# A transformer layer on one Trainium2 core: the last five steps of the kernel by halves of columns, with its final norm rearranged

## The chip, the core and the metric

The kernel runs as one program on one core of a Trainium2 chip. The metric is the device time of one execution in microseconds (us); lower is better. The core's engines work side by side and wait for each other through semaphores: TensorE (PE in the profile; its weight loads are PEld), VectorE (DVE), ScalarE (ACT), GpSimd (POOL) and the queues that issue DMAs. Here SyncE's queue (SP) issues nearly all loads and half of the stores, ACT's queue the other stores.

## The reference

One layer on 1024 frames of width 1024, in float32. Only the last two lines are touched by the change, but the program is one.

```python
h = rms_norm(x, norm1); P = h @ w_in
A = forgetting_attention(...)        # 8 heads, causal, with forget gates
B = chunk_band_attention(...)        # 8 heads, own chunk and 8 before it
x = x + (sigmoid(gA) * (A @ w_a) + sigmoid(gB) * (B @ w_b)) @ w_out
h2 = rms_norm(x, norm2)
x = x + square(relu(h2 @ w_up)) @ w_down       # 1024 -> 4096 -> 1024
return rms_norm(x, final_norm)
# rms_norm(x, g) = x * rsqrt(mean(x * x) + 1e-6) * g, mean over the 1024 features
```

## The kernel before

**Layout.** Activations lie with the features on the 128 partitions and the frames along the free dimension. Frames come in two halves of 512 columns, h = 0 and h = 1 (`HALF = 512`). The output `outT` has eight rows of 128 features; a row of one half is 128x512 floats, 256 KB.

**Exact products.** Every float32 operand is split into a high part (rounded to fp32r) and a low part (the rest), and a product is three matmuls: high by high, high by low, low by high. The high parts are ACT casts (`wh`, `xT4h`), the low part of a weight is a POOL subtraction (`wl`, line 165), that of an activation a DVE subtraction (`xT4l`).

**The down projection** (`w_down`) is the last stage. It is done by Strassen's scheme in seven products in the order of `STEPS`: A11, S1, S2, S3, S4, A12, A22. Each has 16 steps k = 0..15, and a step multiplies one weight quarter (128x512: four blocks m of 128 output features) by one activation tile (128x512): 4 x 3 = 12 matmuls into four PSUM banks `dA22_0..3`. A22 is the last; its activation is T4, read from DRAM (`a_dram`), its weight comes from `wall`.

**Operands of a step** are made by `prepare(s)`: the activation is loaded on SP (`xT`), cast on ACT and subtracted on DVE; then the weight of the step two later (`WLEAD = 2`) is loaded on SP (`wr`); then this step's weight is cast on ACT and subtracted on POOL. From step `GSTEPS` on these instructions keep the order in which they are written on their engines (wrapper class `Ordered`: VO, TO, AO, LO; the profile gives them line 106, the wrapper's line). So the SP queue holds `xT(s), wr(s+2), xT(s+1), wr(s+3)` and so on. There are four buffers for `wr` (`RAW = 4`): the load for step s+2 waits until POOL has subtracted the weight of step s-2. There are six for raw `xT` (`XR`), four each for `xT4h` and `xT4l` (`XB`), six each for `wh` and `wl` (`HL`). `prepare` is called up to three steps ahead (`LEAD`).

**The last steps of A22** are split by columns: with `STAG = 2`, the steps k = 13, 14, 15 are held back and done for the first 256 columns, bank by bank (m = 0..3, three steps each), then for the other 256 columns. After a bank's half: DVE adds it onto `accu` (line 1277), `final` squares the sum on ACT, adds the square onto the running sum on DVE (line 233; the sums lie in `rstd`, named `accs`), and scales `accu` by the norm's gain on ACT (line 1173). Four output rows are in `accu` (tile `au`), four in `accp` (tile `p1`, complete before these steps).

**The final norm of a half of columns** is `finish`: `norm_stat` sums the squares over the partitions by two matmuls with a column of ones (PSUM tile `n_s`), `rms` and `newton` make the inverse root (ACT square root into `n_r`, then small DVE instructions), `spread` copies it to all partitions by two matmuls with the identity (PSUM tile `n_b`), and then eight tiles are multiplied by it and stored. In the first 256 columns of h = 0 POOL multiplies all eight, from an SBUF copy that ACT makes, and SP stores them by pairs; in the second DVE multiplies all eight, straight from PSUM, and SP and ACT take turns to store. The half h = 1 is finished earlier, during A12, with DVE and POOL taking turns; SP's loads for A22 stand behind the first of its stores.

Of the kernel before, what the change touches and what calls it, by code (L numbers as in the profile page):

```python
# [44 lines left out]
LAST_HEAD = "FFFFMWTHTFFFLHFTPLTWPHMLFFWFFTHHLMLTPFFHLTVFXFHLPPMOOTHLOPPOPWVXOO"  # L45
FILL_FROM = 9

LEAD, XB, XR = 3, 4, 6

WLEAD = 2  # L50

STAG = 2

GSTEPS = 4

# [37 lines left out]
def hybrid_block(ctx: ExitStack, tc: tile.TileContext, xT, xN, g1, wall, wf, fb, relb, g2, g3, outT):  # L93
# [28 lines left out]
    def tmp(name, dt=F32):  # L122
        return tp.tile([P, HALF], dt, tag="t", name=name, bufs=8)
# [108 lines left out]
            A.activation(sq, src, AF.Square)  # L232
            eng.tensor_tensor(acc, acc, sq, op=ALU.add)

    def newton(name, v, y, t=None):

        if t is None:
            t = cpool.tile([P, 8], F32, tag="nt", name=f"{name}_t", bufs=2)[:, :v.shape[1]]
        V.reciprocal(y, y)
        V.tensor_tensor(t, v, y, op=ALU.mult)  # L240
        V.tensor_tensor(t, t, y, op=ALU.mult)
        V.tensor_scalar(t, t, -0.5, 1.5, op0=ALU.mult, op1=ALU.add)
        V.tensor_tensor(y, y, t, op=ALU.mult)

    def spread(ps_pool, name, y, eng=T):

# [11 lines left out]
        newton("n1", v, y)  # L258
        return [y[:, 4 * h:4 * h + 4] for h in range(2)]

    def norm_stat(ps_pool, name, acc, eng=T):

        ps = ps_pool.tile([P, HALF], F32, tag="d", name=f"{name}_s")
        n = acc.shape[1] // P
        for c in range(n):
            eng.matmul(ps[:, c:c + 1], acc[:, c * P:(c + 1) * P], ones, start=True, stop=True)
        return rms(name, ps, n)

    def rms(name, ps, n=4):

        y, v, t = cpool.tile([P, 2, 4], F32, tag="nr", name=f"{name}_r", bufs=2)[:, 0, 0:n], ps[:, 8:8 + n], ps[:, 16:16 + n]
        V.tensor_scalar(v, ps[:, 0:n], EPS, None, op0=ALU.add)
        A.activation(y, ps[:, 0:n], AF.Sqrt, bias=epsb)
        newton(name, v, y, t)
        return y

    def split(dst, src, eng):
# [894 lines left out]
        begun.add(h)  # L1172
        A.activation(dst, dst, AF.Copy, scale=gt[:, 2, m + 4 * row:m + 4 * row + 1])

    def finish(ps_pool, h, tiles, engs, q=0, w=HALF):

        cols = slice(q * w, (q + 1) * w)
        eng = T if h else TO
        y = norm_stat(ps_pool, f"n3_{h}{q}", accs[h][:, cols], eng)
        yield  # L1180
        if h:
            yield
        pb = spread(ps_pool, f"n3_{h}{q}", y, eng)[:, 0:w]
        scale = accs[h][:, cols]
        if G in engs:
            A.copy(scale, pb)
        yield
        n = 0
        for row, t in enumerate(tiles):
            for m in range(4):  # L1190
                dst = t[:, m, cols]
                if engs[n % len(engs)] is G:
                    G.tensor_tensor(dst, dst, scale, op=ALU.mult)
                else:
                    V.tensor_tensor(dst, dst, pb, op=ALU.mult)
                out = outT[:, :, h * HALF + q * w:h * HALF + (q + 1) * w]
                if engs != (G,):
                    (load, store)[n % 2](out[:, m + 4 * row, :], dst)
                elif m % 2:
                    load(out[:, m + 4 * row - 1:m + 4 * row + 1, :], t[:, m - 1:m + 1, cols])  # L1200
                n += 1
                yield

    def between(n, banks):

        for m in range(4):
            at = lambda t: t[:, m, :]
            total = lambda t, src: V.tensor_tensor(at(t), banks[m], at(src), op=ALU.add)
            if n == "A11":
                A.copy(at(p1), banks[m])  # L1210
            elif n == "S1":
                total(av, p1)
            elif n == "S2":
                total(au, p1)
                yield
                total(av, av)
            elif n == "S3":
                total(aw, av)
                yield
                total(au, au)  # L1220
            elif n == "S4":
                total(av, av)
                final(av, m, 0, 1)
                yield
                final(aw, m, 1, 1)
            else:
                total(p1, p1)
                final(p1, m, 0, 0)
            yield
        for t, row, h in {"S2": ((p1, 0, 0),), "S3": ((aw, 1, 1), (av, 0, 1), (au, 1, 0))}.get(n, ()):  # L1230
            for m in range(4):
                residual(t, m, row, h)
                if m % 2:
                    yield
        if n == "S4":
            yield from finish(psm[0], 1, (av, aw), (V, G))

    def prepare(s):
        _, n, x, k = steps[s]
# [16 lines left out]
    for s, (i, n, x, k) in enumerate(steps):  # L1256
# [9 lines left out]

        if n == "A22" and k == 15 - STAG:

            for _ in rest:
                pass  # L1270
            rest, w = iter(()), HALF // 2
            for q in range(2):
                cols = slice(q * w, (q + 1) * w)
                for m in range(4):
                    for k in range(15 - STAG, 16):
                        multiply(m, k, cols)
                    V.tensor_tensor(au[:, m, cols], banks[m][:, cols], au[:, m, cols], op=ALU.add)
                    final(au, m, 1, 0, cols)
                    if m % 2:
                        next(rest, None)  # L1280
                for _ in rest:
                    pass
                rest = finish(psm[1], 0, (p1, au), (V,) if q else (G,), q, w)
            break
        for m in range(4):
            multiply(m, k)
# [60 lines left out]
```

## Time and profile before

| | |
|---|---|
| median of 3 runs | 1427.55 us (1426.97 to 1428.85) |
| the profiled execution | 1430.48 us, of which the profile's span is 1428.5 us |
| TensorE busy | 1400.7 us (98% of the span), weight loads 1168.7 us |
| VectorE, ScalarE, GpSimd busy | 885.1 us, 706.6 us, 812.2 us |
| mean granted TensorE clock | 0.995 |
| moved from and to HBM | 172.70 MB read, 85.69 MB written |

Times in the profile are microseconds from the start of the span. A row of the timeline gives the start, the duration, the engine, the source line, the operation, "out<-in" by the program's tile names with buffer numbers left out, and in square brackets how long the engine was idle before and what released it. A busy TensorE is not a TensorE at its peak, since matmuls overlap: what tells its pace is the distance from one start to the next.

### The profile page before, as it was taken

To read this page: it belongs to the slowest core of one execution; us is meant where nothing else is said; L and a number is where in the kernel's file an instruction comes from. 1 tells how busy PE (TensorE), PEld (TensorE's weight loads), DVE (VectorE), ACT (ScalarE), POOL (GpSimd) and SP (SyncE) were. 2 spreads that over 40 slices of the span, in tenths; PEclk is the share of its full clock that TensorE was granted. 3 is DMA by queue.
4 is the path that set the end of the run, shared out by engine and by line. 5 is a ranking of instruction groups with operands and counts; after the bars stand their busy time and mean duration, and the time that the engine had idled before them with its cause. 6 is when DMAs were issued, how large, how long until landed. Compare 5 with 4: busy or idle time off the path is not lost.

```text
span 1428.5 us, 20411 instructions
## 1 busy us (share of the span) xinstructions
PE 1400.7 (98%) x6676; PEld 1168.7 (82%) x6676; DVE 885.1 (62%) x1389; ACT 706.6 (49%) x1361; POOL 812.2 (57%) x639
## 2 busy tenths in 40 slices
PE   9999999999999999999999999999999999999996
PEld 6788888888878888888888888888888888888885
DVE  7756445543258887776655855545555559998644
ACT  8534333343358887775454543333333444444653
POOL 0477777778832233113724677777777545567564
PEclk9999999999999999999999999999999999999998
DMA  8546667773454668886644244444444784678263
GB/s 282 154 116 194 187 196 219 204 198 121 147 169 147 185 209 248 246 257 215 213 162 146 68 166 151 155 154 157 148 154 169 252 269 156 178 234 225 81 221 118
DMA packets 132820, 259.75 MB, mean 182 GB/s; under 512 B 18594, under 2 KB 20642, under 8 KB 129642
## 3 DMA queue, kind: packets, MB, share of 16 engines
q1 hardware_dynamic: 84570, 172.79, 38.6%
q10 hardware_dynamic: 44944, 77.78, 17.2%
q0 software_dynamic: 3200, 7.88, 2.5%
q8 instruction: 52, 0.85, 0.2%
q14 instruction: 54, 0.44, 0.1%
HBM read 172.70 MB, written 85.69 MB: 181 GB/s over the span
## 4 chain that ended last, share of the span: by engine, by line
PE 87%; DVE 3%; issue 3%; ACT 2%; POOL 2%; DMA 2%; SPq 0%; POOLq 0%; ACTq 0%; DVEq 0%
PE u L216 44%; PE dS L216 12%; PE dA L216 5%; PE o L216 5%; PE s L106 5%; PE pv L106 4%; PE pt L106 3%; PE m L106 3%; PE m L216 3%; POOL wl_A L165 1%; PE u L106 1%; DMA xg<-xT 1%; DMA xT<-a_dram 1%; ACT p L106 1%; PE vtp L627 0%
## 5 line engine op out<-in xcount | busy, mean ns | idle before, releaser
L165 POOL TENSOR_TENSOR wl_A<-wr,wh_A 128x512 fp32r<-128x512 f32 x118 | 158.4, 1352 | 94.0 <-ACT wh_A L163 77.0
L165 POOL TENSOR_TENSOR wl_S<-S,wh_S 128x512 fp32r<-128x512 f32 x102 | 136.0, 1337 | 32.9 <-ACT wh_S L163 32.3
L163 ACT CAST wh_S<-S 128x512 fp32r<-128x512 f32 x105 | 64.6, 621 | 114.0 <-PE u L216 53.9
L163 ACT CAST wh_A<-wr 128x512 fp32r<-128x512 f32 x105 | 65.0, 620 | 88.7 <-PE u L216 55.8
L106 DVE TENSOR_TENSOR tl<-pt,th 128x512 fp32r<-128x512 f32 (+1 forms) x144 | 90.5, 641 | 25.9 <-ACT th L106 24.4
L165 POOL TENSOR_TENSOR wl_S<-ks,wh_S 128x512 fp32r<-128x512 f32 x48 | 69.1, 1501 | 53.4 <-ACT wh_S L106 50.0
L590 DVE TENSOR_TENSOR u<-u,u 128x512 f32<-128x512 f32 x70 | 48.8, 698 | 76.0 <-PE u L216 73.6
L106 ACT ACTIVATE p<-s,mn 128x640 f32<-128x640 f32 (+3 forms) x120 | 84.4, 703 | 16.6 <-DVE mn L106 15.5
L106 ACT CAST th<-pt 128x512 fp32r<-128x512 f32 (+1 forms) x144 | 77.6, 551 | 24.5 <-PE pt L106 22.3
L106 PE MATMUL pt<-ident,p 128*128 128x128 f32 x528 | 78.1, 274 | 1.2 <-DVE zt L403 1.1
L186 POOL TENSOR_TENSOR S<-wr,wr 128x512 f32<-128x512 f32 x35 | 46.3, 1324 | 54.8 <-DMA wr<-wall 50.2
L106 PEld LDWEIGHTS pt<-ident,p 128*128 128x128 f32 x528 | 62.2, 141 | 11.0 <-PE pv L106 2.0
L106 PE MATMUL s<-qk 128*128 128x384 f32 (+2 forms) x192 | 58.6, 360 | 8.1 <-ACT p L106 7.3
L165 POOL TENSOR_TENSOR wl_A<-ka,wh_A 128x512 fp32r<-128x512 f32 x32 | 45.1, 1419 | 35.6 <-ACT wh_A L106 34.1
L278 ACT CAST qkh<-qk 128x512 fp32r<-128x512 f32 x32 | 19.9, 621 | 87.5 <-DMA qk_dram<-qkl 34.2
L1102 ACT ACTIVATE v<-v 128x512 f32<-128x512 f32 x64 | 40.4, 632 | 45.1 <-DVE v L1101 42.9
L924 POOL TENSOR_TENSOR on<-on,lo 128x512 f32<-128x512 f32 x7 | 9.0, 1292 | 92.7 <-ACT lo L106 92.7
L106 PE MATMUL pv<-th,v 128*128 128x512 f32 (+3 forms) x180 | 61.3, 348 | 0.1
L583 DVE TENSOR_TENSOR u<-u,c 128x512 f32<-128x512 f32 x35 | 24.5, 699 | 59.4 <-PE u L216 57.3
L106 PE MATMUL pv<-tl,v 128*128 128x512 f32 (+3 forms) x180 | 56.8, 335 | 0.2 <-DVE tl L106 0.2
L1101 DVE SCALAR_TENSOR_TENSOR v<-u,rstd 128x512 f32<-128x512 f32 x64 | 43.9, 688 | 20.1 <-PE u L216 18.1
L581 DVE TENSOR_TENSOR c<-u,u 128x512 f32<-128x512 f32 x35 | 24.2, 691 | 50.7 <-PE u L216 48.9
(445 smaller groups left out, 4742.2 us busy)
## 6 DMA issues: line engine op xcount, KB each, us to landing
wr<-wall SPq DMA_DIRECT2D x233, 256.0 KB
a_dram<-at ACTq DMA_DIRECT2D x64, 256.0 KB
xT<-a_dram SPq DMA_DIRECT2D x64, 256.0 KB
qk<-qk_dram SPq DMA_DIRECT2D x15, 1024.0 KB
qk_dram<-qkh ACTq DMA_DIRECT2D x96, 128.0 KB
a_dram<-v ACTq DMA_DIRECT2D x48, 256.0 KB
xB<-a_dram SPq DMA_DIRECT2D x44, 256.0 KB
z_dram<-zt ACTq DMA_DIRECT2D x32, 256.0 KB
```

The source lines that it names most:

```text
L106: return lambda *a, **kw: tc.keep_in_program_order(getattr(self.eng, name)(*a, **kw))
L163: (act.tensor_copy if act is G or act is V else act.copy)(wh, src)
L165: lows.append(eng.tensor_tensor(wl, src, wh.bitcast(F32), op=ALU.subtract))
L186: eng.tensor_tensor(t, raw(3), raw(2), op=ALU.add)
L216: done = eng.matmul(bank, w[wi], x[xi], start=(first and t == 0), stop=(t == n - 1 and not part), skip_group_check=part or not first)
L278: A.copy(dst[0], src)
L581: V.tensor_tensor(c22, banks[2], u2, op=ALU.add)
L583: V.tensor_tensor(banks[1], banks[3], c22, op=ALU.add)
L590: V.tensor_tensor(banks[b], banks[b], u2, op=ALU.add)
L924: G.tensor_tensor(o, o, lows_o[pr], op=ALU.add)
L1101: V.scalar_tensor_tensor(v, src, 0.0, rstd[:, hs(h)], op0=ALU.max, op1=ALU.mult)
L1102: A.activation(v, v, AF.Square)
```

## The change

Six things change at once.

1. `STAG` goes from 2 to 4: the steps k = 11 to 15 are done by halves of columns, so five steps per bank instead of three, 120 matmuls of 256 columns instead of 72, and 24 fewer of 512. All five steps' operands must be held at once, and `XB` goes from 4 to 5.
2. The square of the last bank (m = 3) of each half is no longer added onto the running sum on DVE; its sum over the partitions is added in PSUM by two more matmuls with the ones (`more` in `norm_stat`).
3. The first half's inverse root is spread while TensorE is in the second half's bank m = 2, not after the last product. POOL multiplies the four tiles of `accp` and DVE the four of `accu`; the stores are by pairs, one of them on ACT's queue.
4. The second half is multiplied by DVE (six tiles) and POOL (two), after an ACT copy, and stored in five DMAs.
5. `newton` takes four DVE instructions instead of five, in all norms; the epsilon is added after the square root on ACT has been issued, and the mean lies in SBUF.
6. Four matmuls with the identity (`spin`) stand between the second half's sums and its spread.

```diff
@@ -45,11 +45,11 @@
 LAST_HEAD = "FFFFMWTHTFFFLHFTPLTWPHMLFFWFFTHHLMLTPFFHLTVFXFHLPPMOOTHLOPPOPWVXOO"
 FILL_FROM = 9
 
-LEAD, XB, XR = 3, 4, 6
+LEAD, XB, XR = 3, 5, 6
 
 WLEAD = 2
 
-STAG = 2
+STAG = 4
 
 GSTEPS = 4
 
@@ -232,15 +232,14 @@
             A.activation(sq, src, AF.Square)
             eng.tensor_tensor(acc, acc, sq, op=ALU.add)
 
-    def newton(name, v, y, t=None):
+    def newton(name, v, y, t=None, vec=V):
 
         if t is None:
             t = cpool.tile([P, 8], F32, tag="nt", name=f"{name}_t", bufs=2)[:, :v.shape[1]]
-        V.reciprocal(y, y)
-        V.tensor_tensor(t, v, y, op=ALU.mult)
-        V.tensor_tensor(t, t, y, op=ALU.mult)
-        V.tensor_scalar(t, t, -0.5, 1.5, op0=ALU.mult, op1=ALU.add)
-        V.tensor_tensor(y, y, t, op=ALU.mult)
+        vec.reciprocal(y, y)
+        vec.tensor_tensor(t, y, y, op=ALU.mult)
+        vec.scalar_tensor_tensor(t, t, -0.5, v, op0=ALU.mult, op1=ALU.mult)
+        vec.scalar_tensor_tensor(y, t, 1.5, y, op0=ALU.add, op1=ALU.mult)
 
     def spread(ps_pool, name, y, eng=T):
 
@@ -258,20 +257,23 @@
         newton("n1", v, y)
         return [y[:, 4 * h:4 * h + 4] for h in range(2)]
 
-    def norm_stat(ps_pool, name, acc, eng=T):
+    def norm_stat(ps_pool, name, acc, eng=T, more=None):
 
         ps = ps_pool.tile([P, HALF], F32, tag="d", name=f"{name}_s")
         n = acc.shape[1] // P
-        for c in range(n):
-            eng.matmul(ps[:, c:c + 1], acc[:, c * P:(c + 1) * P], ones, start=True, stop=True)
-        return rms(name, ps, n)
-
-    def rms(name, ps, n=4):
-
-        y, v, t = cpool.tile([P, 2, 4], F32, tag="nr", name=f"{name}_r", bufs=2)[:, 0, 0:n], ps[:, 8:8 + n], ps[:, 16:16 + n]
-        V.tensor_scalar(v, ps[:, 0:n], EPS, None, op0=ALU.add)
+        for t in (acc,) if more is None else (acc, more):
+            for c in range(n):
+                eng.matmul(ps[:, c:c + 1], t[:, c * P:(c + 1) * P], ones, start=more is None or (t is acc and c == 0),
+                           stop=more is None or t is more, skip_group_check=more is not None)
+        return rms(name, ps, n, V if more is None else VO)
+
+    def rms(name, ps, n=4, vec=V):
+
+        r = cpool.tile([P, 2, 4], F32, tag="nr", name=f"{name}_r", bufs=2)
+        y, v = r[:, 0, 0:n], r[:, 1, 0:n]
         A.activation(y, ps[:, 0:n], AF.Sqrt, bias=epsb)
-        newton(name, v, y, t)
+        vec.tensor_scalar(v, ps[:, 0:n], EPS, None, op0=ALU.add)
+        newton(name, v, y, ps[:, 16:16 + n], vec)
         return y
 
     def split(dst, src, eng):
@@ -1172,32 +1174,24 @@
         begun.add(h)
         A.activation(dst, dst, AF.Copy, scale=gt[:, 2, m + 4 * row:m + 4 * row + 1])
 
-    def finish(ps_pool, h, tiles, engs, q=0, w=HALF):
-
-        cols = slice(q * w, (q + 1) * w)
-        eng = T if h else TO
-        y = norm_stat(ps_pool, f"n3_{h}{q}", accs[h][:, cols], eng)
+    def finish(ps_pool, h, tiles):
+
+        y = norm_stat(ps_pool, f"n3_{h}", accs[h], T)
         yield
-        if h:
-            yield
-        pb = spread(ps_pool, f"n3_{h}{q}", y, eng)[:, 0:w]
-        scale = accs[h][:, cols]
-        if G in engs:
-            A.copy(scale, pb)
+        yield
+        pb = spread(ps_pool, f"n3_{h}", y, T)
+        scale = accs[h]
+        A.copy(scale, pb)
         yield
         n = 0
         for row, t in enumerate(tiles):
             for m in range(4):
-                dst = t[:, m, cols]
-                if engs[n % len(engs)] is G:
+                dst = t[:, m, :]
+                if n % 2:
                     G.tensor_tensor(dst, dst, scale, op=ALU.mult)
                 else:
                     V.tensor_tensor(dst, dst, pb, op=ALU.mult)
-                out = outT[:, :, h * HALF + q * w:h * HALF + (q + 1) * w]
-                if engs != (G,):
-                    (load, store)[n % 2](out[:, m + 4 * row, :], dst)
-                elif m % 2:
-                    load(out[:, m + 4 * row - 1:m + 4 * row + 1, :], t[:, m - 1:m + 1, cols])
+                (load, store)[n % 2](outT[:, m + 4 * row, h * HALF:(h + 1) * HALF], dst)
                 n += 1
                 yield
 
@@ -1233,7 +1227,7 @@
                 if m % 2:
                     yield
         if n == "S4":
-            yield from finish(psm[0], 1, (av, aw), (V, G))
+            yield from finish(psm[0], 1, (av, aw))
 
     def prepare(s):
         _, n, x, k = steps[s]
@@ -1268,19 +1262,62 @@
 
             for _ in rest:
                 pass
-            rest, w = iter(()), HALF // 2
+            while len(ready) < len(steps):
+                ready.append(prepare(len(ready)))
+            rest, w, tiles, lasts, ys, pbs = iter(()), HALF // 2, (p1, au), [], [], []
+
+            def spin(n):
+                bank = psm[1].tile([P, HALF], F32, tag="d", name="spin")
+                for _ in range(n):
+                    TO.matmul(bank[:, 0:P], ident, ident, start=True, stop=True)
+
+            def stat(q):
+                ys.append(norm_stat(psm[1], f"n3_0{q}", accs[0][:, q * w:(q + 1) * w], TO, lasts[q]))
+
+            def wide(q):
+                pbs.append(spread(psm[1], f"n3_0{q}", ys[q], TO)[:, 0:w])
+
+            def spare(q):
+                A.copy(accs[0][:, q * w:(q + 1) * w], pbs[q])
+
+            def scaled(q, row, ms, eng, queue):
+                cols = slice(q * w, (q + 1) * w)
+                for m in ms:
+                    t = tiles[row][:, m, cols]
+                    eng.tensor_tensor(t, t, accs[0][:, cols] if eng is G else pbs[q], op=ALU.mult)
+                queue(outT[:, 4 * row + ms[0]:4 * row + ms[-1] + 1, cols], tiles[row][:, ms[0]:ms[-1] + 1, cols])
+
             for q in range(2):
                 cols = slice(q * w, (q + 1) * w)
                 for m in range(4):
                     for k in range(15 - STAG, 16):
                         multiply(m, k, cols)
+                        if (q, m, k) == (1, 2, 16 - STAG):
+                            wide(0)
+                            spare(0)
                     V.tensor_tensor(au[:, m, cols], banks[m][:, cols], au[:, m, cols], op=ALU.add)
-                    final(au, m, 1, 0, cols)
-                    if m % 2:
-                        next(rest, None)
-                for _ in rest:
-                    pass
-                rest = finish(psm[1], 0, (p1, au), (V,) if q else (G,), q, w)
+                    if m < 3:
+                        final(au, m, 1, 0, cols)
+                    else:
+                        lasts.append(tmp("sq")[:, 0:w])
+                        A.activation(lasts[q], au[:, m, cols], AF.Square)
+                        A.activation(au[:, m, cols], au[:, m, cols], AF.Copy, scale=gt[:, 2, 7:8])
+                    if q and m == 0:
+                        stat(0)
+                    if q and m == 2:
+                        for ms in ((0, 1), (2, 3)):
+                            scaled(0, 0, ms, G, load)
+            scaled(0, 1, (0, 1), VO, store)
+            scaled(0, 1, (2, 3), VO, load)
+            stat(1)
+            spin(4)
+            wide(1)
+            spare(1)
+            scaled(1, 0, (0, 1), VO, load)
+            scaled(1, 1, (2, 3), G, load)
+            scaled(1, 0, (2, 3), VO, store)
+            scaled(1, 1, (0,), VO, load)
+            scaled(1, 1, (1,), VO, store)
             break
         for m in range(4):
             multiply(m, k)
```

The first place is TensorE where A22's steps go over to halves of columns (`xT4h13` is the high part of the activation of step 13, `wl_A22_13` the low part of its weight, `dA22_0` the bank of m = 0). Before:

```order
L106 MATMUL dA22_3_13924<-xT4h12_14149,wl_A22_12_14157 128x512
L106 MATMUL dA22_0_13921<-xT4h13_14173,wh_A22_13_14179 128x256
L106 MATMUL dA22_0_13921<-xT4l13_14174,wh_A22_13_14179 128x256
L106 MATMUL dA22_0_13921<-xT4h13_14173,wl_A22_13_14181 128x256
L106 MATMUL dA22_0_13921<-xT4h14_14197,wh_A22_14_14201 128x256
L106 MATMUL dA22_0_13921<-xT4l14_14198,wh_A22_14_14201 128x256
L106 MATMUL dA22_0_13921<-xT4h14_14197,wl_A22_14_14203 128x256
L106 MATMUL dA22_0_13921<-xT4h15_14219,wh_A22_15_14223 128x256
L106 MATMUL dA22_0_13921<-xT4l15_14220,wh_A22_15_14223 128x256
L106 MATMUL dA22_0_13921<-xT4h15_14219,wl_A22_15_14225 128x256
L106 MATMUL dA22_1_13922<-xT4h13_14173,wh_A22_13_14179 128x256
```

The whole matmuls of step 12 stand ahead of the first half, and step 15 is the third of the halves. The same engine and place in the changed kernel, from the second matmul of step 12 (the three of step 11 and the first of step 12, all 128x256, stand right ahead of it, and ahead of those the whole matmuls of step 10):

```order
L106 MATMUL dA22_0_13917<-xT4l12_14146,wh_A22_12_14151 128x256
L106 MATMUL dA22_0_13917<-xT4h12_14145,wl_A22_12_14153 128x256
L106 MATMUL dA22_0_13917<-xT4h13_14169,wh_A22_13_14175 128x256
L106 MATMUL dA22_0_13917<-xT4l13_14170,wh_A22_13_14175 128x256
L106 MATMUL dA22_0_13917<-xT4h13_14169,wl_A22_13_14177 128x256
L106 MATMUL dA22_0_13917<-xT4h14_14193,wh_A22_14_14197 128x256
L106 MATMUL dA22_0_13917<-xT4l14_14194,wh_A22_14_14197 128x256
L106 MATMUL dA22_0_13917<-xT4h14_14193,wl_A22_14_14199 128x256
L106 MATMUL dA22_0_13917<-xT4h15_14203,wh_A22_15_14207 128x256
L106 MATMUL dA22_0_13917<-xT4l15_14204,wh_A22_15_14207 128x256
L106 MATMUL dA22_0_13917<-xT4h15_14203,wl_A22_15_14209 128x256
L106 MATMUL dA22_1_13918<-xT4h11_14121,wh_A22_11_14127 128x256
```

The product of step 15 for the bank m = 0 now stands ahead of all products of steps 11 to 14 for the other banks. The orders of SP, ACT, DVE and POOL from A22's first operand to its last are those of before.

The second place is ScalarE at the program's end, from the last square (`sq`) on. Before, and then changed:

```order
L232 ACTIVATE sq_14358<-accu_11375 128x256
L1173 ACTIVATE accu_11375<-accu_11375,gt_77 128x256
L1186 COPY rstd_80<-n3_00_b_14362 128x256
L273 ACTIVATE n3_01_r_14381<-n3_01_s_14378,epsb_73 128x2
L1198 DMA outT<-accp1_11374 128x256 x2
L1198 DMA outT<-accu_11375 128x256 x2
```

```order
L1303 ACTIVATE sq_14388<-accu_11372 128x256
L1304 ACTIVATE accu_11372<-accu_11372,gt_77 128x256
L1288 DMA outT<-accu_11372 128x2x256
L274 ACTIVATE n3_01_r_14402<-n3_01_s_14397,epsb_73 128x2
L1281 COPY rstd_80<-n3_01_b_14414 128x256
L1288 DMA outT<-accp1_11371 128x2x256
L1288 DMA outT<-accu_11372 128x256
```

(`n3_00` is the norm of the first 256 columns, `n3_01` that of the second; `_s` the sums, `_r` the inverse roots, `_b` the spread.) A store of the first half now stands ahead of the second half's square root, and the copy after its spread is new. On VectorE at the same place, from the last bank's addition on in the changed kernel:

```order
L1298 TENSOR_TENSOR accu_11372<-dA22_3_13920,accu_11372 128x256
L106 TENSOR_TENSOR accu_11372<-accu_11372,n3_00_b_14348 128x256 x4
L106 TENSOR_SCALAR n3_01_r_14402<-n3_01_s_14397 128x2
L106 RECIPROCAL n3_01_r_14402<-n3_01_r_14402 128x2
L106 TENSOR_TENSOR n3_01_s_14397<-n3_01_r_14402 128x2
L106 SCALAR_TENSOR_TENSOR n3_01_s_14397<-n3_01_s_14397,n3_01_r_14402 128x2
L106 SCALAR_TENSOR_TENSOR n3_01_r_14402<-n3_01_s_14397,n3_01_r_14402 128x2
L106 TENSOR_TENSOR accp1_11371<-accp1_11371,n3_01_b_14414 128x256 x4
L106 TENSOR_TENSOR accu_11372<-accu_11372,n3_01_b_14414 128x256 x2
```

Before, six small instructions stood there, and then four multiplications of `accp1` and four of `accu`, both by the second half's spread.

## The prediction

> **What bounds the kernel now.** I read the page first, then the waits over the last product A22, then the timelines of its last steps and of the end.
>
> ```profile
> span 1428.5 us, 20411 instructions
> PE 1400.7 (98%) x6676; PEld 1168.7 (82%) x6676; DVE 885.1 (62%) x1389; ACT 706.6 (49%) x1361; POOL 812.2 (57%) x639
> ```
>
> TensorE is busy nearly throughout, so only its waits, and what follows its last product, can be won or lost. First its pace, and where it waits near the end:
>
> ```profile
> 1396.90 0.39 PE L106 MATMUL dA<-xT4h,wh_A 128*128 128x512 f32 x1
> ...
> 1405.06 0.28 PE L106 MATMUL dA<-xT4h,wh_A 128*128 128x256 f32 x1
> ...
> 1407.21 0.38 PE L106 MATMUL dA<-xT4h,wl_A 128*128 128x256 f32 x1 [0.74 <-POOL wl_A L165]
> 1407.43 0.28 PE L106 MATMUL dA<-xT4h,wh_A 128*128 128x256 f32 x1
> 1407.55 0.28 PE L106 MATMUL dA<-xT4l,wh_A 128*128 128x256 f32 x1
> ...
> 1415.34 0.28 PE L106 MATMUL dA<-xT4h,wl_A 128*128 128x256 f32 x1
> 1416.60 0.71 PE L106 MATMUL n_b<-ident,n_r 128*128 128x128 f32 x4 [0.98 <-DVE n_r L243]
> 1417.15 0.52 PE L106 MATMUL n_s<-ones,rstd 128*128 128x1 f32 x4
> 1419.22 0.71 PE L106 MATMUL n_b<-ident,n_r 128*128 128x128 f32 x4 [1.55 <-DVE n_r L243]
> ```
>
> The first row is the first of step 10 (from it on the program order is kept), the second the first of step 13, where the halves begin: 36 matmuls in 8.16 us, 0.227 us each, 2.72 us a step. The halves go at 0.12 us a matmul. The third row is the ninth of the 72: step 15's low weight came late. The last product ends at 1415.62 (call it T0); the span goes on for 12.9 us. What made step 15 late:
>
> ```profile
> ACT xT4h L106 <- DMA xT<-a_dram: 10.8, 7, 3.3
> ACT xT4h L106 <- PE dA L216: 2.6, 2, 1.4
> PEld dA L106 <- POOL wl_A L165: 0.9, 1, 0.9
> PEld dA L106 <- DVE xT4l L106: 0.2, 1, 0.2
> ...
> SPq L106 <- POOL wl_A L165: 17.5, 10, 3.3
> ```
>
> The first four are waits from 1370 to 1408, the last SP's own from 1360 to 1410. The casts wait for loads (7 times), hardly for TensorE to free a buffer (2), and the loads wait in SP's queue for POOL's subtraction (10 times, 17.5 us), which frees a raw weight buffer. The last turn of that loop, from three timelines:
>
> ```profile
> 1397.17 4.71 POOL L165 TENSOR_TENSOR wl_A<-wr,wh_A 128x512 fp32r<-128x512 f32 x3 [2.99 <-ACT wh_A L106]
> ...
> 1398.50 0.33 SPq L106 DMA_DIRECT2D wr<-wall  x1
> 1398.92 0.86 SPq L106 DMA_DIRECT2D xT<-a_dram  x2
> ...
> 1402.97 0.62 ACT L106 CAST xT4h<-xT 128x512 fp32r<-128x512 f32 x1 [3.30 <-DMA xT<-a_dram]
> ...
> 1404.02 0.62 ACT L106 CAST xT4h<-xT 128x512 fp32r<-128x512 f32 x1
> ...
> 1405.44 1.71 POOL L165 TENSOR_TENSOR wl_A<-wr,wh_A 128x512 fp32r<-128x512 f32 x1
> ```
>
> When POOL has finished step 11 (the first of the three), SP issues the last weight load and, behind it, the activations of steps 14 and 15. They are cast 4.05 us after their issue, and step 15's low weight is ready at 1407.15. TensorE is not in this loop.
>
> **Part 1: five steps by halves.** No number of buffers in the loop changes: raw weights stay at four. The fifth `xT4h` buffer removes only a wait for TensorE, and of the two waits so named (2.6 us) neither is in the rows above. So step 15 is again ready near 1407.2. The first half's spread of h = 1 stands two matmuls earlier, which may start A22's loads 2 x 0.227 = 0.45 us sooner; I take that whole. But the first bank's products of step 15 now stand ahead of all the other banks' of steps 11 to 14: TensorE reaches the halves at 1405.06 - 2 x 2.72 = 1399.62 and wants step 15 after 12 matmuls, at 1401.1. It waits, with a few matmuls between, until 1407.2 - 0.45, some 6 us; queued behind it are the products of steps 11 to 14 for the other three banks, whose operands are there, and DVE and ACT wait for their sums. Until 1407.21 the old kernel has done 9 of 72 half matmuls and its whole steps; the new one has 105 to go, not 63: 42 x 0.12 = 5.0 us later. Inside the second half stand the sums, now of four matmuls instead of two (the row at 1417.15 has two in 0.52 us; two more 0.3) and the spread (from 1416.60 to the next start, 0.55). T0 moves by 5.0 + 0.3 + 0.55 - 0.45 = +5.4 us. Bounds: 0 if operands come in time; 6.5 if the loop is a microsecond later. I take 5.4, since every row of the loop is untouched.
>
> **The clock.** In the 6 us of waiting TensorE does about ten half matmuls. What that does to its clock:
>
> ```profile
> 7.29 1.22 PE L371 MATMUL g<-B11h,wh_g 128*128 128x512 f32 x2 [1.65 <-ACT B11h L278]
> ...
> 9.48 0.63 PE L371 MATMUL g<-B11l,wh_g 128*128 128x512 f32 x1
> 9.91 0.63 PE L371 MATMUL g<-B11h,wl_g 128*128 128x512 f32 x1
> ...
> 10.76 0.40 PE L386 MATMUL f<-B11l,T4h 128*40 128x512 f32 x1
> ...
> 1420.40:1420.50 0.10, 0.00 (x0) 0.00 (x0) 0.10 (x1) 0.00 (x0) 0.10 (x1) 0.74 1.03 348
> ```
>
> At the program's start a 512-column matmul takes 0.43 us from start to start instead of 0.227 (half pace) and 0.63 us by itself; the row at 10.76 is the first with the short duration. In the last row, a window of the stages, the granted clock (0.74, then lower) drops 0.5 us after the spread at 1419.22, though the 4.8 us before it held three short groups, 1.9 us. The wait in the new kernel is as sparse, so I take a drop: a 256-column matmul then takes 0.213 us. At the start full pace came 3.5 us after dense work began (7.29 to 10.76), so one such stretch costs 3.5 x (1 - 0.12/0.213) = 1.5 us; I take 1.3, since part of it passes in the wait. Bounds 0 and 2.8 (two stretches).
>
> The Trainium skill, page "TensorE: Matmul & The Clock Gate", section "Why this matters for your kernels", asks for no idle gap over about 3 us between bursts. Each gap here is about 2 us or less, so by that rule the clock would stay, and the sum would be 1.3 us lower (the second case below). The row at 1420.40 speaks against it: the longest wait in those 4.8 us is 1.55 us.
>
> **Parts 2 to 5: the end behind T0.**
>
> ```profile
> 1415.66 0.42 DVE L1277 TENSOR_TENSOR accu<-dA,accu 128x256 f32<-128x256 f32 x1 [0.38 <-PE dA L106]
> ...
> 1416.12 0.42 ACT L232 ACTIVATE sq<-accu 128x256 f32<-128x256 f32 x1
> 1416.57 0.51 ACT L1173 ACTIVATE accu<-accu,gt 128x256 f32<-128x256 f32 x1
> 1417.35 0.37 ACT L1186 COPY rstd<-n_b 128x256 f32<-128x256 f32 x1 [0.28 <-PE n_b L106]
> 1417.91 0.26 ACT L273 ACTIVATE n_r<-n_s,epsb 128x2 f32<-128x2 f32 x1 [0.19 <-DVE n_s L272]
> 1420.76 1.02 ACTq L1198 DMA_DIRECT2D outT<-accp  x2
> ...
> 1418.81 0.17 DVE L242 TENSOR_SCALAR n_s<-n_s 128x2 f32<-128x2 f32 x1
> 1419.01 0.16 DVE L243 TENSOR_TENSOR n_r<-n_r,n_s 128x2 f32<-128x2 f32 x1
> 1419.97 1.42 DVE L1195 TENSOR_TENSOR accp<-accp,n_b 128x256 f32<-128x256 f32 x4 [0.80 <-PE n_b L106]
> 1421.30 1.41 DVE L1195 TENSOR_TENSOR accu<-accu,n_b 128x256 f32<-128x256 f32 x4
> ...
> 1417.80 2.77 POOL L1193 TENSOR_TENSOR accp<-accp,rstd 128x256 f32<-128x256 f32 x4 [10.64 <-ACT rstd L1186]
> ...
> GB/s 304 188 306 60 0 157 154 222 345 48 0 10 0 0 0 0 0 0 0 0 0 0 0 0 0 0 0 0 0 134 175 264 341 339 341 343 348 193 0 0
> ```
>
> Before: first multiplication at T0 + 4.35, last ended at T0 + 7.1. The last row is the DMA traffic from 1395 to 1429 in 0.85 us slices: all 2 MB of the half go out in one stretch, at 341 GB/s when it runs, until about 1427.0; the span ends 1.5 us later. Stores set the end.
>
> After, from T0: addition to 0.46, square to 0.9, sums to 1.5. ACT scales until 1.4 and then issues a first-half store (half of 1.02 us), which waits for two of VectorE's multiplications (0.46 + 2 x 0.34 = 1.15, so not held up): the square root ends near 2.2 instead of 1.8. Five DVE steps at 0.2 (1418.81 to 1419.01) end at 3.25; the spread and its latency (1419.22 to 1419.97, 0.75, and 0.05 ahead) make 4.05; the ACT copy, for which DVE now waits, 0.4: 4.45. So the shorter root and the sums in PSUM win nothing on this path; queue and copy eat it. `spin` costs nothing, hidden behind the root (1.5 to 3.25). Six multiplications at 0.34 end at 6.5, POOL's two beside them.
>
> The gain is the store of the first half. Its spread stands 24 matmuls (2.9 us) ahead of T0, so that POOL, after spread and copy, multiplies `accp` from about T0 - 2.1 to T0 + 0.7 (2.77 us for four), and DVE `accu` until 1.85: four stores issued from -0.7 to 1.9, 1 MB at 341 GB/s, out by about 5. The other 1 MB starts at 4.45 + 0.7 + 0.6 (issue to data) = 5.75 and takes 3.1 us at 341 GB/s, or 4.2 with the ramp of the quoted row (134, 175, 264): end at 5.75 + 3.1 to 4.2 + 1.5 = 10.4 to 11.5, not 12.9. Gain 1.4 to 2.5; I take 2.0. The shorter root also saves one 0.2 us step where TensorE waits for the first norm, near the program's start; the second norm's root has no such wait:
>
> ```profile
> PE n_b L249 <- DVE n1r L243: 1.2, 1, 1.2
> ```
>
> **Sum**: +5.4 + 1.3 - 2.0 - 0.2 = +4.5 us. The sum is against the profiled execution (1430.48 us, span 1428.5), which lies 2.9 above the median 1427.55; on the median it gives 1432.0.
>
> **The cases.**
> - Forecast: operands late, clock falls. +4.5, 1432.0; own range 1430.2 to 1433.8 (loop within a microsecond, tail 1.4 to 2.5).
> - Operands late, clock holds: +3.2, 1430.7. For it: there are matmuls between the gaps; against: the drop at 1420.40. Decided by the pitch behind the wait, 0.12 or 0.21.
> - Not slower: operands in time. If the two waits for TensorE that the fifth buffer removes started the whole loop earlier, and it kept the lead, the 1.2 us of waits today go too (0.9 in the row of PEld, 0.24 ahead of step 15's low activation); 24 more half matmuls for 12 whole cost 2 x (24 x 0.12 - 12 x 0.227) = 0.3, sums and spread 0.85: T0 - 0.05, and with tail and first norm -2.25, 1425.3. It decides from an operand 6 us earlier; against it stands the loop, where loads, not TensorE, release the casts.
> - Worse: clock down for two such stretches, or the last stores slower: +5.4 + 2.8 - 1.4 - 0.2 = +6.6, 1434.1.
>
> **Chances.** 0.41, 0.25, 0.24, 0.10. About 0.2% (2.9 us) can be told from no change: slower from 1430.4, faster below 1424.7. The second case falls half on each side of 1430.4 (0.12 same, 0.13 slower); the third spreads by its tail and loop: 0.13 faster, 0.11 same. Faster 0.13, same 0.23, slower 0.64. The range takes in the third case's centre and the fourth's: 1425.0 to 1434.0.
>
> **What would show it.** Right: a wait of TensorE for `wl_A` or `xT4l` of several us in all near 1400 to 1407; the granted clock below 1 soon after; T0 near 1422; first multiplication of the second half 4.4 us behind T0; the end some 11 us behind T0. Wrong, if TensorE has no wait there, or if step 15's subtraction on POOL ends well before 1406.

## The result and the profile after

The changed kernel took 1439.98 us (median of 4 runs, 1438.78 to 1441.29), the kernel before 1428.20 us beside it (4 runs, 1426.97 to 1429.68): ratio 1.0078 (changed to before), 95% interval 1.0066 to 1.0090. It is slower by 11 us, where 4.5 us were predicted. The profiled execution took 1438.78 us, its span is 1437.1 us.

**Where the time went.** The windows of 50 us of TensorE alone, laid side by side, agree within 0.6 us in both kernels but for two places: the end, and one window that the prediction never looked at, 1100 to 1150 us, where TensorE was busy for 50.0 us before and 45.55 us after. That is where the up projection ends and the down projection's first product, A11, begins. First the timeline of before there, TensorE and POOL:

```profile
1106.13 0.39 PE L216 MATMUL u<-T4h,wl_A 128*128 128x512 f32 x1
1106.36 0.39 PE L216 MATMUL dA<-xB11h,wh_A 128*128 128x512 f32 x1
...
1096.19 0.54 POOL L1145 DMA_DIRECT2D ka<-wall  x1
1097.30 1.06 POOL L1145 DMA_DIRECT2D ka<-wall  x2 [0.58 <-PE u L216]
1099.80 0.54 POOL L1145 DMA_DIRECT2D ka<-wall  x1 [1.43 <-PE u L216]
1100.33 2.62 POOL L163 CAST wh_A<-ka 128x512 fp32r<-128x512 f32 x3
```

POOL issues the loads of A11's first four weight tiles (`ka`) 10.2 to 6.6 us before A11, and A11 follows the last product without a gap. The same place after:

```profile
1104.05 0.39 PE L216 MATMUL u<-T4h,wl_A 128*128 128x512 f32 x1
1108.89 0.79 PE L216 MATMUL dA<-xB11h,wh_A 128*128 128x512 f32 x1 [4.45 <-POOL wh_A L163]
1109.48 0.63 PE L216 MATMUL dA<-xB11l,wh_A 128*128 128x512 f32 x1
1109.90 0.63 PE L216 MATMUL dA<-xB11h,wh_A 128*128 128x512 f32 x1
...
1103.37 2.13 POOL L1147 DMA_DIRECT2D ka<-wall  x4 [9.49 <-PE u L216]
1108.13 0.70 POOL L163 CAST wh_A<-ka 128x512 fp32r<-128x512 f32 x1 [2.63 <-DMA ka<-wall]
```

POOL stood 9.49 us for a product of `u` and issued all four loads together from 1103.37 on, while the last product's last matmuls ran; 4.8 us later the first tile was there and could be cast. TensorE idled 4.45 us, and then started from one matmul to the next in 0.43 us instead of 0.227. How long that lasted, from windows of TensorE (length, busy time with the number of matmuls, granted clock, DMA share, GB/s):

```profile
1105.00:1108.00 3.00, 0.00 (x0) 0.95 0.64 173
1108.00:1110.00 2.00, 1.11 (x3) 0.50 0.95 330
1110.00:1112.00 2.00, 2.00 (x6) 0.50 1.02 394
1112.00:1114.00 2.00, 2.00 (x6) 0.50 1.02 369
1114.00:1116.00 2.00, 2.00 (x9) 0.87 0.79 209
```

The clock was at 0.50 for some 6 us. (The stage before A11 differs by up to 2 us from one execution to the next, whatever the kernel: A11 starts between 1104.18 and 1106.44 in all executions without this stall. So the stages behind are compared from A11's start on.)

**Why POOL waited.** The pools are stacked in SBUF in this order, and a buffer waits for whatever lay at its address before:

```python
    xq = pool(ctx, "xq", "left")           # xT4h, xT4l: XB buffers each, 2 KB per partition
    xr = pool(ctx, "xr", "left")           # raw xT: XR buffers
    hp = {"a": pool(ctx, "ka", "left")}    # the held weights of A11
```

`XB` from 4 to 5 makes `xq` 2 x 2 KB longer, and `ka` moves up by 4 KB. The program of POOL shows what that does to the first two loads (in brackets the semaphores that each waits for: VectorE's, TensorE's, those of earlier loads), before and after:

```
494 L1145 DMA ka_11390<-wall 128x512
495 L1145 DMA ka_11392<-wall 128x512 [waits DMASW0_49,PE_49]
```

```
494 L1147 DMA ka_11387<-wall 128x512 [waits DVE_49,PE_49]
495 L1147 DMA ka_11389<-wall 128x512 [waits DMASW0_49]
```

Before, `ka0` had nothing to wait for. After, it lies on the high part of an operand tile T4 of the up projection and waits for VectorE's subtraction that read it and for its last reader on TensorE, one of that projection's last twelve matmuls; the three loads behind it on POOL's queue wait with it.

**The end** is what the prediction spoke of. The halves after, TensorE (the prediction's third row, step 15's low product, answers to the one at 1410.32):

```profile
1404.71 0.28 PE L106 MATMUL dA<-xT4h,wh_A 128*128 128x256 f32 x1
...
1408.65 0.58 PE L106 MATMUL dA<-xT4h,wl_A 128*128 128x256 f32 x1 [0.76 <-POOL wl_A L165]
...
1410.32 0.58 PE L106 MATMUL dA<-xT4h,wl_A 128*128 128x256 f32 x1 [0.55 <-POOL wl_A L165]
1410.70 0.42 PE L106 MATMUL dA<-xT4h,wh_A 128*128 128x256 f32 x1
1410.92 0.41 PE L106 MATMUL dA<-xT4l,wh_A 128*128 128x256 f32 x1
...
1415.06 0.28 PE L106 MATMUL dA<-xT4h,wh_A 128*128 128x256 f32 x1
1415.18 0.28 PE L106 MATMUL dA<-xT4l,wh_A 128*128 128x256 f32 x1
...
1426.33 0.28 PE L106 MATMUL dA<-xT4h,wl_A 128*128 128x256 f32 x1
```

Step 15 came late, as forecast; behind it the pitch (from one start to the next) was 0.21 us until 1414.8 and 0.12 from then on; T0 is 1426.61. The end behind it, from four timelines:

```profile
1427.05 1.40 DVE L106 TENSOR_TENSOR accu<-accu,n_b 128x256 f32<-128x256 f32 x4
1430.67 1.42 DVE L106 TENSOR_TENSOR accp<-accp,n_b 128x256 f32<-128x256 f32 x4 [1.27 <-ACT rstd L1281]
...
1430.26 0.37 ACT L1281 COPY rstd<-n_b 128x256 f32<-128x256 f32 x1 [1.73 <-PE n_b L106]
...
1424.37 3.02 POOL L1287 TENSOR_TENSOR accp<-accp,rstd 128x256 f32<-128x256 f32 x4 [14.10 <-ACT rstd L1281]
...
1428.09 1.14 PE L106 MATMUL spin<-ident 128*128 128x128 f32 x8
1429.54 0.68 PE L106 MATMUL n_b<-ident,n_r 128*128 128x128 f32 x4 [0.31 <-DVE n_r L106]
```

The first half is scaled on POOL from T0 - 2.24 on, the second half's first multiplication starts at T0 + 4.06, and the span ends 1437.1 - 1426.61 = 10.5 us behind T0 (12.9 before).

### The profile page after: what moved, and what is told of

Read it like the earlier page. It is cut to its first block, busy times and chain, and to the rows that moved or that the text cites. A ratio compares the mean times of both kernels' runs of the same rounds, so it can differ in the third digit from the quotient of the medians.

```text
span 1437.1 us, 20476 instructions
## 1 busy us (share of the span) xinstructions
PE 1407.5 (98%) x6716; PEld 1174.6 (82%) x6716; DVE 890.2 (62%) x1383; ACT 707.0 (49%) x1362; POOL 812.4 (57%) x637
## 4 chain that ended last, share of the span: by engine, by line
PE 88%; DVE 4%; ACT 2%; issue 2%; DMA 2%; POOL 1%; SPq 0%; ACTq 0%; DVEq 0%; POOLq 0%
PE u L216 44%; PE dS L216 12%; PE dA L216 6%; PE o L216 5%; PE s L106 5%; PE pv L106 4%; PE pt L106 3%; PE m L106 3%; PE m L216 3%; POOL wl_A L165 1%; PE u L106 1%; PE dA L106 1%; DMA xg<-xT 1%; DMA xT<-a_dram 1%; ACT p L106 1%
```

## The experiments

Ratios are to the kernel before, run beside each experiment; its median there was 1428.49 to 1429.10 us, while the expectations start from 1428.2 or 1428.5. So the ratios are what to compare, and differences in microseconds are worked out from them.

**The address.** Two kernels tell it from everything else in the change. One is the kernel before with nothing but a 4 KB gap below `ka`:

```diff
+    pool(ctx, "gap", "left").tile([P, 2, HALF], F32, tag="gap", name="gap")
     hp = {"a": pool(ctx, "ka", "left")}
```

> The kernel before, with an empty tile of 4 KB per partition ahead of the pool `ka`, as much as the fifth `xT4h` and `xT4l` buffers take in the changed kernel; nothing else. Theory 1 (addresses): `ka0` then lies on an operand tile `T4` that the up-projection's last product still reads; its load, on POOL's queue, and the three behind it wait for that product, TensorE stands some 4.5 us ahead of A11 and then runs some 2 us slower at the lowered clock: 1428.2 + 6.5 = 1434.7 us (1433 to 1436.5). Rival (the loss comes from the earlier casts and subtractions that a fifth buffer allows, or from the halves alone): 1428.2 us, within 1 us, no wait ahead of A11.

1437.45 us, ratio 1.0057 (1.0044 to 1.0069), or 8.1 us slower (6.3 to 9.9). Its timeline of POOL and TensorE has the stall to the hundredth:

```profile
1105.30 2.12 POOL L1146 DMA_DIRECT2D ka<-wall  x4 [9.27 <-PE u L216]
...
1110.81 0.79 PE L216 MATMUL dA<-xB11h,wh_A 128*128 128x512 f32 x1 [4.45 <-POOL wh_A L163]
```

From A11's start to the first 256-column product it needs 1412.38 - 1110.81 = 301.6 us, the kernel before 1405.06 - 1106.36 = 298.7: 2.9 us for the lowered clock. Stall and clock make 7.3 us up to there. Some of it is won back in the halves, where TensorE no longer waits for step 15: T0 is 310.97 us behind A11's start, against 309.26 before, and the two profiled spans differ by 1434.5 - 1428.5 = 6.0 us, near the 6.5 expected. These two executions lie closer together than the medians do (1436.33 - 1430.48 = 5.9 us, against 8.1); what makes up the rest stays open.

As a control, the same gap above all these pools, which takes the memory but moves no buffer:

```diff
     sums("v", "w")
+    pool(ctx, "gap", "left").tile([P, 2, HALF], F32, tag="gap", name="gap")
```

> The kernel before with the same empty 4 KB per partition, now above `ka`, `ks` and the sums instead of below them: as much memory, no buffer moved. Theory 1 (only the place of `ka` counts): 1428.5 us, within 0.8 us, no wait ahead of A11. Rival (the extra memory itself, or any change to this part of the program, costs it): 1433 us or more.

1428.36 us, ratio 0.9997 (0.9988 to 1.0005), no wait ahead of A11. The place costs, not the memory. In the programs, `ka0` waits for the same two things in the kernel with the gap below as in the changed kernel, and for nothing with the gap above, as before.

The other way round, the changed kernel with `ka` where it had been:

```diff
     sums("v", "w")
+    xr2 = pool(ctx, "xr2", "left")
...
-        raw = xr.tile([P, HALF], F32, tag="xr", name=f"x{x}{k}", bufs=XR)
+        raw = (xr, xr2)[s % 6 > 3].tile([P, HALF], F32, tag="xr", name=f"x{x}{k}", bufs=(4, 2)[s % 6 > 3])
```

> The changed kernel, with two of the six raw `xT` buffers moved to a pool above the sums, so that `ka` lies again where it lay before. Theory 1: no wait ahead of A11, 1440.0 - 6.5 = 1433.5 us (1432 to 1435), which is the prediction's own sum with a somewhat larger loss of clock. Rival: the halves carry the loss, 1440 us, within 1.5 us.

1433.29 us, ratio 1.0028 (1.0017 to 1.0039): 4.0 us slower than before (2.4 to 5.6), where the prediction's sum was 4.5. Of the 11 us, 7 are the address. TensorE after that repair:

```profile
1104.38 0.39 PE L216 MATMUL dA<-xB11h,wh_A 128*128 128x512 f32 x1
...
1398.67 0.38 PE L106 MATMUL dA<-xT4h,wl_A 128*128 128x256 f32 x1 [0.26 <-POOL wl_A L165]
1400.02 0.38 PE L106 MATMUL dA<-xT4h,wh_A 128*128 128x256 f32 x1 [0.97 <-ACT wh_A L106]
...
1401.38 0.58 PE L106 MATMUL dA<-xT4h,wl_A 128*128 128x256 f32 x1 [0.76 <-POOL wl_A L165]
...
1403.05 0.58 PE L106 MATMUL dA<-xT4h,wl_A 128*128 128x256 f32 x1 [0.54 <-POOL wl_A L165]
1403.43 0.41 PE L106 MATMUL dA<-xT4h,wh_A 128*128 128x256 f32 x1
...
1408.12 0.29 PE L106 MATMUL dA<-xT4l,wh_A 128*128 128x256 f32 x1
...
1419.28 0.28 PE L106 MATMUL dA<-xT4h,wl_A 128*128 128x256 f32 x1
```

A11 follows without a wait. Step 15's low product starts at 1403.05, 298.7 us behind A11's start (before: 1407.21, 300.9); the half pace lasts until 1408.1; T0 is 1419.56.

**The clock behind the waits.** The same kernel with 25 extra products of step 11, into a bank that nothing reads, put where TensorE waits:

```diff
+                        if (q, m) == (0, 0) and k > 12:
+                            fill(FILL[k][0])      # 0, 8, 0 products ahead of steps 13, 14, 15
...                                                # the step's two products with wh
+                            fill(FILL[k][1])      # 3, 6, 8 ahead of its product with wl
```

> As the run with `ka` back (1433.3 us), with 25 extra products of step 11 into an unused bank, put where TensorE waits for steps 13 to 15 in the first half. They change no operand's time. If the loss behind the waits is the clock, lowered because TensorE works too sparsely while it waits: the pitch stays at 0.12 us, T0 comes up to 3 us sooner, 1430.5 us (1429.8 to 1431.5). Rival (the low clock follows the waits for another reason, or the extra work delays the products as much as it saves): 1433 us or more, the pitch of 0.213 us remains.

```profile
1403.64 1.11 PE L106 MATMUL fill<-xT4h,wh_A 128*128 128x256 f32 x8
1404.58 0.36 PE L106 MATMUL dA<-xT4h,wl_A 128*128 128x256 f32 x1
1404.78 0.28 PE L106 MATMUL dA<-xT4h,wh_A 128*128 128x256 f32 x1
1404.90 0.28 PE L106 MATMUL dA<-xT4l,wh_A 128*128 128x256 f32 x1
...
1418.56 0.28 PE L106 MATMUL dA<-xT4h,wl_A 128*128 128x256 f32 x1
```

From the windows of all engines (length; busy time with the number of instructions of TensorE, its weight loads, VectorE, ScalarE and GpSimd; granted clock; DMA share; GB/s), without the extra products and then with them:

```profile
1400.00:1402.00 2.00, 1.22 (x5) 0.95 (x5) 1.52 (x2) 1.01 (x2) 1.95 (x2) 0.83 0.02 4
1402.00:1404.00 2.00, 1.46 (x6) 1.16 (x6) 0.33 (x1) 0.00 (x0) 0.99 (x1) 0.50 0.00 0
```

```profile
1400.00:1402.00 2.00, 1.15 (x9) 0.93 (x8) 0.70 (x2) 1.70 (x4) 0.48 (x1) 1.00 0.05 20
1402.00:1404.00 2.00, 1.88 (x14) 1.48 (x13) 1.36 (x1) 0.49 (x1) 2.00 (x2) 1.00 0.01 4
```

With 23 matmuls in these 4 us instead of 11 the granted clock stays at 1.00. The pitch behind the waits is 0.12 us, and from step 15's low product to T0 it takes 1418.84 - 1404.58 = 14.26 us, against 1419.56 - 1403.05 = 16.51: the clock had cost 2.25 us. The whole is 1431.18 us, ratio 1.0018 (1.0009 to 1.0028), some 1.4 us better by the ratios, whose intervals overlap; in the profiled execution most of the 2.25 is gone, because step 15 came 1.4 us later (1404.58 - 1104.48 = 300.1 us behind A11's start, not 298.7) and because the end behind T0 is 0.4 us longer (the second half's spread took 1.11 us instead of 0.68). What moves the loop by 1.4 us between two executions was not found.

**Operands in time.** A22's raw weights get six buffers of their own, above the sums:

```diff
         if n == "A22":
-            return quarter(u, 2, ld)
+            q = xw.tile([P, HALF], F32, tag="xw", name=f"xw{k}", bufs=6)
+            ld(q, wall[u, :, 2, :])
+            return q
```

> As the run with `ka` back, and A22's raw weights in six buffers of their own instead of the four shared ones. If the four raw buffers are what makes step 15 late (the loop of the prediction): no wait in the halves, no loss of clock there, T0 up to 7 us sooner: 1426 to 1429 us. Rival (the loop starts late because of the norm of h = 1, or is bound by the loads themselves): 1432 to 1434 us, the waits for `wl_A` in the halves remain.

1427.25 us, ratio 0.9988 (0.9980 to 0.9997): now faster than before, by 1.7 us (0.4 to 2.9). One wait is left, the clock stays:

```profile
1400.36 0.39 PE L106 MATMUL dA<-xT4h,wl_A 128*128 128x256 f32 x1 [0.75 <-POOL wl_A L165]
1400.58 0.28 PE L106 MATMUL dA<-xT4h,wh_A 128*128 128x256 f32 x1
1400.70 0.27 PE L106 MATMUL dA<-xT4l,wh_A 128*128 128x256 f32 x1
```

T0 is 1414.64, 309.9 us behind A11's start, against 315.2 with four buffers and 309.3 before. So the four shared raw buffers did make step 15 late, as the prediction read from SP's waits. That the new ones are two more, and that they are A22's own, was not told apart.

**The parts apart.** The halves without the new end and root (the kernel before with `STAG = 4`, `XB = 5`, all operands prepared ahead of the halves, and `ka` in place by the edit above, left out here):

```diff
-LEAD, XB, XR = 3, 4, 6
+LEAD, XB, XR = 3, 5, 6
-STAG = 2
+STAG = 4
+            while len(ready) < len(steps):
+                ready.append(prepare(len(ready)))
```

> The kernel before with five steps by halves, five `xT4` buffers and `ka` at its old place: part 1 of the prediction alone, without the new end and the shorter root. By the prediction's sum (T0 +5.4, clock +1.3 by it and 2.5 by the trace, no gain at the end): 1428.5 + 6.7 to 7.9 = 1435.2 to 1436.4 us. Rival: the longer second half alone lets the old end's first half finish beside it, so that the new end is worth nothing: 1433.3 us, within 0.8 us.

1433.61 us, ratio 1.0036 (1.0024 to 1.0049). In microseconds that is below the 1435.2 to 1436.4 expected and the rival's number, but against 1.0028 with the new end the intervals overlap, and 2 us between the two are not excluded. In its trace T0 is 1420.05, 314.7 us behind A11's start (315.2 with the new end, whose sums and spread lie inside the second half), and the span ends 12.3 us behind T0 (10.4). From A11's start to the end the two executions differ by 1.3 us, but step 15's low product came 1.1 us later in this one (299.8 us behind A11's start, not 298.7). So what the new end is worth beside five steps is not settled; 0.6 us of the 2.4 by which the end behind T0 became shorter come from the longer second half alone (12.9 to 12.3).

The new end and root without the longer halves:

```diff
-LEAD, XB, XR = 3, 5, 6
+LEAD, XB, XR = 3, 4, 6
-STAG = 4
+STAG = 2
```

> The changed kernel with three steps by halves and four buffers as before (STAG 2, XB 4): the store of the first half beside the second, the sums in PSUM and the shorter root remain. By the prediction's parts 2 to 5: T0 as before apart from the sums and spread inside the second half (+0.85), the end 2.4 us sooner behind T0: 1428.2 - 1.5 = 1426.7 us (1425.5 to 1427.7). Rival: with three steps the second half is too short to cover the first half's scaling on POOL, and the gain behind T0 is eaten: 1428 to 1429.5 us.

1428.22 us, ratio 0.9994 (0.9985 to 1.0003): no difference that can be told. T0 is 309.5 us behind A11's start, as before, and the end 11.5 us behind T0, not 10.5. That is the rival's case more than the expected one: the last addition onto the running sum takes 0.89 us, the sums wait 0.82 us for it, and the second half's first multiplication comes at T0 + 5.15 (4.04 in the repaired kernel). With six raw buffers in addition (same edit as above):

> Three steps by halves, four `xT4` buffers, the new end, and A22's raw weights in six buffers of their own. With three steps TensorE waits only 0.3 us for step 15 as it is, so by the prediction's loop there is little left to win: 1428.0 us (1427.2 to 1428.6). Rival (whatever made the five-step run 6 us faster with six buffers does so here): 1426 us or less.

1427.85 us, ratio 0.9993 (0.9984 to 1.0002). With three steps there was no late operand to cure, as expected.

**Four steps, six raw buffers**, `ka` in place:

```diff
-STAG = 4
+STAG = 3
```

> Four steps by halves with the new end, `ka` back and six raw buffers for A22. If with operands in time the number of steps only trades the cost of halves (12 more 256-column products per step and half, 0.15 us a step) against cover for the first half's scaling: 1427.2 us (1426.5 to 1428.0), between the runs with three and five. Rival (four is the point where both waits vanish): 1426.0 us or less.

1426.28 us, ratio 0.9983 (0.9975 to 0.9992): between the expected range and the rival's. The interval overlaps those with three steps (0.9993) and with five (0.9988), so that four is the best number is not shown. TensorE has no wait for an operand left in the halves; T0 is 1414.23, 308.6 us behind A11's start, the end 10.9 behind T0.

**The `spin` products.** With three steps they ended behind the root, and the spread behind them. TensorE in the run with three steps and six raw buffers, then in the same without `spin`:

```profile
1417.08 2.06 PE L106 MATMUL spin<-ident 128*128 128x128 f32 x8
1418.92 1.06 PE L106 MATMUL n_b<-ident,n_r 128*128 128x128 f32 x4
```

```profile
1418.90 1.22 PE L106 MATMUL n_b<-ident,n_r 128*128 128x128 f32 x4 [1.22 <-DVE n_r L106]
```

```diff
-            spin(4)
```

> The run with three steps and six raw buffers without the four `spin` products. There they ended after the root, so that the spread stood behind them. If they cost what they are in the way: the spread comes 0.5 us sooner, first multiplication of the second half near T0 + 5.0 instead of 5.57, 1427.3 us (1426.8 to 1427.9). Rival (they hold the clock up): without them the spread runs slower by as much, 1427.9 us or more.

1426.79 us, at the lower edge of what was expected, ratio 0.9988 (0.9979 to 0.9996); the first multiplication comes at T0 + 5.09 instead of 5.57, as expected. The step of the total from 0.9993 is within the intervals.

> The run with four steps and six raw buffers without the four `spin` products. There they ended before the root. If they only fill an idle stretch: 1426.3 us, within 0.6 us, first multiplication at T0 + 4.4. Rival (they hold the clock up for the spread): the spread at half pace already when it starts, T0 + 4.8 or later, 1426.8 us or more.

1426.18 us, ratio 0.9982 (0.9973 to 0.9991), the first multiplication at T0 + 4.51 (4.48 with `spin`), the spread in 1.22 us instead of 1.09. So the rival's slower spread is there, but it costs 0.03 us. With three and four steps `spin` buys nothing that can be measured; with five, where the spread behind it took 0.68 us, it was not taken out. The kernels with four steps and six raw buffers, with `spin` and without, are faster than the kernel before by 2.4 us (1.1 to 3.6) and 2.6 (1.3 to 3.9).

## Why the prediction was wrong, and where it held

**The step that failed** is the fifth buffer in part 1: "The fifth `xT4h` buffer removes only a wait for TensorE". It was priced as a wait gone and never as 4 KB that push the pools above it onto other tiles. The cost, 4.45 us of idle TensorE and 2.9 us of low clock, stands 300 us ahead of the steps for which the buffer was added; no case held it, the widest stopped at 1434.1, and "What would show it" named only the last stage. The program of POOL shows it: a load that had no wait had one for TensorE, with three more queued behind it. The gap alone, the control and the repair show it from three sides; 4.0 (repaired) and 8.1 (gap alone) add up to the 11.1 measured within their intervals.

Without that term the sum came out: +4.5 predicted, +4.0 (2.4 to 5.6) measured in the repaired kernel. That it came so close is partly luck, since two terms missed in opposite directions. Its terms, from A11's start on in the repaired kernel's trace:

| term | predicted | trace |
|---|---|---|
| step 15's operands against before | 0.45 us sooner | 300.9 - 298.7 = 2.2 sooner (0.8 in the filled run) |
| 42 more products behind them, sums, spread | 5.0 + 0.3 + 0.55 = 5.85 | 14.26 - 8.41 = 5.85 (filled run, against 1415.62 - 1407.21) |
| clock | 1.3 (0 to 2.8) | 2.25 |
| T0 in all | 6.7 | 315.2 - 309.3 = 5.9 |
| end behind T0 | -2.0 (-1.4 to -2.5) | 10.4 - 12.9 = -2.4 |
| first norm | -0.2 | its wait 1.0 us, not 1.2: -0.2 (1.1 in the changed kernel) |
| sum | +4.5 | 5.9 - 2.4 - 0.2 = +3.3 by this trace, +4.0 by the runs |

- **The halves.** The mechanism, all of step 15 wanted in the first bank while a POOL-fed loop of four raw buffers sets its time, is shown by the six-buffer run. Two sizes were off in opposite directions: the loop came 2.2 us sooner, not 0.45, and the clock cost 2.25 us, not 1.3. The half pace lasted some 7 us from the first slow product, not 3.5.
- **The clock.** In the repaired kernel the longest distance between two starts is 1.35 us (1398.67 to 1400.02), and the pace fell; filling those gaps kept it. The Trainium skill, page "TensorE: Matmul & The Clock Gate", section "Why this matters for your kernels", asks for no idle gap over about 3 us between bursts. Keeping to that was not enough here. Whether the length of a single gap or the share of work over some stretch decides was not told apart, since the extra products change both. The second case (clock holds, +3.2) was thus refuted, and its difference to the forecast under-priced: 2.25, not 1.3.
- **The rival on the other side**, operands in time, was priced at -2.25 us. The six-buffer kernel is this case: -1.7 (0.4 to 2.9 faster). It was a good account of what the change could be, and rightly less likely than the forecast with the loop untouched.
- **The end.** First multiplication at T0 + 4.06 (predicted 4.45, before 4.35), POOL from T0 - 2.24 (2.1 predicted), the end 10.5 (10.4 to 11.5). That queue and ACT copy eat what the shorter root wins holds but for 0.3 us. That `spin` is hidden holds with five steps, where it ends at 1429.23 and the root at 1429.40; with three it does not.

## What to carry to other kernels

One more buffer in a pool moves every pool stacked above it. Compare the waits of the first loads of each such pool before and after, on the queue that issues them, before pricing anything else; if one has gained a wait, put the extra buffers above what must load early. Splitting more steps for the sake of overlap pulls their operands' due time forward: widen the feed first (here by six raw buffers of the last product's own), then choose the number of steps; here three, four and five lay within their intervals of each other once the feed was wider.

## What the runs showed of the hardware

- A stall of 4.45 us cost another 2.9 us of half pace behind it, in two kernels alike. TensorE lost its pace also in a stretch of short products with at most 1.35 us from one start to the next (granted clock 0.83, then 0.50, in the repaired kernel).
- VectorE's addition of two SBUF tiles onto the running sum (line 233) takes 0.42 us, but 1.03 us in the changed kernel and 1.02 us in the repaired one where POOL multiplies SBUF tiles beside it; its additions that read one operand from PSUM keep their 0.42 us there. In the changed kernel, without and with POOL at work (POOL's row of four multiplications is at 1424.37):

```profile
1423.52 0.42 DVE L233 TENSOR_TENSOR rstd<-rstd,sq 128x256 f32<-128x256 f32 x1 [0.48 <-ACT sq L232]
1425.76 1.03 DVE L233 TENSOR_TENSOR rstd<-rstd,sq 128x256 f32<-128x256 f32 x1 [0.48 <-ACT sq L232]
```
